# One layer-wide change in an encoder kernel: eight casts of w_out are issued behind the exponentials of the first head group

## The chip, the core and the metric

One core of a Trainium2 chip runs the whole program once. The metric is the device time of one execution in microseconds (us); the median of several runs counts. TensorE (PE) multiplies matrices, VectorE (DVE), ScalarE (ACT) and GpSimd (POOL) work element by element, and SyncE (SP) issues most of the loads and stores. Each engine takes its instructions strictly in the order in which they stand in its queue and waits for semaphores of the others.

## What is computed

The reference is a two-layer encoder over 1024 tokens of width 1024. Each layer mixes three groups of channels, and then applies a gated feed-forward network:

```python
y_f = _fourier_mix(zf, w_fourier[l])                       # 256 channels
y_a = _window_attn(q, k, v, sink[l])                       # 8 heads, 2 key heads, blocks of 128
y_m = _memory_attn(zm.reshape(b, s, N_MEM_HEADS, HEAD_DIM), km, vm)   # 4 heads, 256 memory rows
y = jnp.concatenate([_rmsnorm(y_f, gg[:256]), _rmsnorm(y_a, gg[256:768]), _rmsnorm(y_m, gg[768:])], -1) @ w_out[l]
x = x + _rmsnorm(y, g_post_mix[l])
gate, up = jnp.split(_rmsnorm(x, g_pre_ffn[l]) @ w_ffn_in[l], 2, axis=-1)
x = x + _rmsnorm((jax.nn.silu(gate) * up) @ w_ffn_out[l], g_post_ffn[l])
```

All inputs are 32-bit floats. Rows 256 to 767 of w_out (1024 x 1024) are those that the window attention's output is multiplied with.

## The kernel before

Every product is made from split operands: a matrix is cast to the shorter type that TensorE reads fast (`hi`) on ScalarE, and VectorE or GpSimd computes the remainder (`lo`); three matmuls then stand for one. The sequence is cut in 8 tiles of 128 tokens.

The code is written as lists of units that `weave` interleaves, and a scheduler then orders the instructions of each engine from a model of their durations; so the order on each engine is not that of the text. Large buffers are slices of two arenas (`arena_f` for 32-bit floats, `arena_r` for the short type) that the text places by hand, small ones and PSUM tiles come from pools.

The stages of a layer around the change, in order: the q projection woven with the memory attention (`mem_units`: score matmuls `ms`, VectorE row maxima L842, scaling of them L843, exponentials L846, reciprocals L850, GpSimd scaling of the probabilities L852, transposes `mpT`, casts L151 with remainders L152, products with the values `mav`, and their fold L876, L877); then the first head group of the window attention (`att_units(0)`: matmuls `sc`, masked maxima L729, four exponentials L741 and a small one for the sink L746, a GpSimd scaling L752, transposes `pT`, products `av`) woven with `fm_units`, which multiply the Fourier and memory parts with their rows of w_out (`mo`) and store the sums to `pmd`; then the second head group (`att_units(1)`) together with `out`, which multiplies the attention's output with rows 256 to 767 of w_out (also `mo`), adds `pmd` and goes on to the feed-forward network.

`load_wout` brings rows of w_out in: for each row block of 128 and each half of 512 columns one load (L909) into one of three buffers `raws`, one ScalarE cast with the gain (L910) and one VectorE pass for the remainder (L911). `fm_load` calls it for 4 row blocks that `fm_units` needs (tiles `big`), `out_load` for the row blocks 2 to 5, that is rows 256 to 767 (tiles in `arena_r`). Each call makes 8 loads, 8 casts and 8 passes. `values_32` (L791) rebuilds V for the second head group with two GpSimd additions; its output takes the place in `arena_f` of one of the buffers of `raws`.

Of the kernel before, what the change touches and what calls it, by code (L numbers as in the profile page):

```python
# [2 lines left out]

# [1 line left out]

# [10 lines left out]
AF = mybir.ActivationFunctionType  # L16
# [6 lines left out]
NT = S // P  # L23
# [35 lines left out]
def weave(*streams):  # L59

    order = []
    for si, units in enumerate(streams):
        order += [((i + 0.5) / len(units), si, i, u) for i, u in enumerate(units)]
    for *_, u in sorted(order, key=lambda o: o[:3]):
        u()
# [3 lines left out]
def tile_encoder(ctx: ExitStack, tc: tile.TileContext, T, C, out):  # L69
    nc = tc.nc  # L70
# [11 lines left out]
    def nm(s):  # L82
        uid[0] += 1
        return f"{s}_{uid[0]}"
# [15 lines left out]
    def at(k, *shape, dt=F32):  # L100

        o = int(k * 256)
        ap = arenas[F32R if dt is F32R else F32][:, o : o + math.prod(shape)]
        return shaped(ap.bitcast(dt) if dt is I32 else ap, shape)

    def big(*shape, dt=F32R):

        return bp.tile([P, *shape], dt, tag="big", name=nm("big"))
# [29 lines left out]
    def sm(n, name="v"):  # L138
        if name not in smp:
            smp[name] = ctx.enter_context(tc.tile_pool(name="sm_" + name, bufs=N_SM.get(name, 4)))  # L140
        return smp[name].tile([P, n], F32, tag=name, name=nm(name))

    def ps(shape, name="ps", tag="pd"):
        return psp[tag].tile([P] + list(shape), F32, tag=tag, name=nm(name))
# [323 lines left out]
    class Mix:  # L468
# [248 lines left out]
        def att_scores(self, g, n):  # L717
            k0, k1 = max(0, n - 1), min(NT, n + 2)
            W = (k1 - k0) * P
            m0 = (k0 - (n - 1)) * P  # L720
            half, c = divmod(n, 4)
            es_ = [es_ring(2, 3 * P) for _ in range(2)]
            rmax = sm(4, "rmax")
            for h in range(4):
                pt = ps([W], "sc", "sc")
                lhs = self.qst[half][h % 2][:, 2 * g + h // 2, c * P : c * P + P]
                for i in range(2):
                    mm(pt, lhs, self.kst[g][i][:, k0 * P : k1 * P], start=i == 0, stop=i == 1)  # L728
                nc.vector.tensor_tensor_reduce(  # L729
                    out=es_[h // 2][:, h % 2, :W], in0=pt, in1=mask[:, m0 : m0 + W], op0=ALU.add, op1=ALU.max,  # L730
                    scale=1.0, scalar=-3e38, accum_out=rmax[:, h : h + 1],
                )
            hs = slice(4 * g, 4 * g + 4)
            nmx = sm(4, "nmx")
            nc.vector.scalar_tensor_tensor(
                out=nmx, in0=rmax, scalar=-QK_SCALE, in1=nsink[:, self.l, hs], op0=ALU.mult, op1=ALU.min
            )
            den = sm(4, "den")
            for h in range(4):
                eh = es_[h // 2][:, h % 2, :W]  # L740
                nc.scalar.activation(  # L741
                    eh, eh, AF.Exp, bias=nmx[:, h : h + 1], scale=QK_SCALE, accum_out=den[:, h : h + 1]
                )
            es = sm(4, "es")
            nc.vector.tensor_tensor(out=es, in0=nmx, in1=psink[:, self.l, hs], op=ALU.add)
            nc.scalar.activation(es, es, AF.Exp)  # L746
            nc.vector.tensor_tensor(out=den, in0=den, in1=es, op=ALU.add)
            rden = sm(4, "rden")
            nc.vector.reciprocal(rden, den)
            for h in range(4):  # L750
                eh = es_[h // 2][:, h % 2, :W]
                nc.gpsimd.tensor_scalar(  # L752
                    out=eh, in0=eh, scalar1=rden[:, h : h + 1], scalar2=1.0, op0=ALU.mult, op1=ALU.mult
                )
            return es_
# [48 lines left out]
        def att_units(self, g):  # L804

            self.ya = getattr(self, "ya", {})
            st = {}

            def unit(i):
                if SKEW <= i < NT + SKEW:  # L810
                    n = i - SKEW
                    half, c = divmod(n, 4)
                    if g == 0 and n == 0:
                        ya = at(8, 2, 2, 512)
                        self.ya[0, 0], self.ya[0, 1] = ya[:, 0], ya[:, 1]
                    if g == 0:
                        dst = self.ya[g, half][:, :, c * P : c * P + P]
                    else:
                        dst = self.ya[g, n] = y1s(2, P)
                    self.att_values(g, n, st.pop(n), dst)  # L820
                    if g:
                        self.out_prep(n)
                if i < NT:
                    st[i] = self.att_scores(g, i)

            return [lambda i=i: unit(i) for i in range(NT + SKEW)]
# [69 lines left out]
            return [lambda i=i: unit(i) for i in range(n + 2)]  # L896


        def load_wout(self, ks, k0=None):

            res = {}
            for j, k in enumerate(ks):
                w = big(2, D) if k0 is None else at(k0 + 8 * j, 2, D, dt=F32R)
                hi, lo = w[:, 0], w[:, 1]
                g = ggT[:, self.l * NK + k : self.l * NK + k + 1]
                for n in range(2):
                    ns = slice(n * 512, n * 512 + 512)
                    raw = raws(512)
                    nc.sync.dma_start(raw, T["w_out"][self.l, k * P : (k + 1) * P, ns])  # L909
                    nc.scalar.activation(hi[:, ns], raw, AF.Copy, scale=g)  # L910
                    nc.vector.scalar_tensor_tensor(  # L911
                        out=lo[:, ns], in0=raw, scalar=g, in1=f32(hi[:, ns]), op0=ALU.mult, op1=ALU.subtract
                    )
                res[k] = (hi, lo)
            return res
# [59 lines left out]
            return [lambda t=t: unit(t) for t in range(NT)]  # L975

        def out_load(self):
            self.woa = self.load_wout((2, 3, 4, 5), 32)

        def out_gains(self):  # L980
            self.gpost = gain(T["g_post_mix"][self.l], at(48, D))
# [321 lines left out]
    mix = Mix(0, hT, mem)  # L1303
# [13 lines left out]
    for l in range(DEPTH):  # L1317
# [7 lines left out]
        mem.load()  # L1325
        weave(mix.mem_units(), q[4:8] + [mix.fm_load] + q[8:])
        fm = mix.fm_units(pmd)
        weave(mix.att_units(0), fm[:6] + [mix.out_load] + fm[6:])
        mix.out_gains()
        xs = x_in if l == 0 else x2d  # L1330
        hb = Blocks()
# [44 lines left out]
        if l + 1 < DEPTH:  # L1376
            mem = Memory(l + 1, 16, 0, 16, 28, "pT")
            mix = Mix(l + 1, nhT, mem)
# [76 lines left out]
```

## Time and profile before

| | us |
|---|---|
| median of 3 runs | 2131.66 |
| lowest and highest run | 2131.02, 2137.23 |
| profiled execution, its time | 2135.5 |
| its span in the trace | 2133.7 |
| TensorE busy | 2013.2 |
| VectorE, ScalarE, GpSimd busy | 1577.7, 1060.6, 863.4 |

The profiled execution is one run with the hardware profiler on; its span is what the trace covers. A busy share is an average over stages with different limits, so it is to be read by stage. The granted clock is a share of 2.4 GHz: 0.50 is the lower level of 1.2 GHz, and a mean between tells how much of a stretch ran at which.

### The profile page before, as it was taken

How to read it: one execution, taken by the hardware profiler on the slowest of the kernel's cores; microseconds unless marked ns; L12 is line 12 of the kernel's file. 1: busy time of each engine (PE TensorE's matmuls, PEld its weight loads, DVE VectorE, ACT ScalarE, POOL GpSimd, SP SyncE). 2: the span in 40 equal slices, each digit the busy share in tenths (PEclk: the TensorE clock that was granted, in tenths of full speed). 3: DMA queues.
4: the chain of work that ended last, by engine and by line, in shares of the span. 5: the costliest groups of instructions: out<-in, count | busy, mean ns of one | idle time of the engine just before them, and what ended most of it. 6: DMA issues, size and time to landing. Idle time of an engine off the chain costs nothing.

```text
span 2133.7 us, 28334 instructions
## 1 busy us (share of the span) xinstructions
PE 2013.2 (94%) x9490; PEld 1655.0 (78%) x9490; DVE 1577.7 (74%) x2441; ACT 1060.6 (50%) x2257; POOL 863.4 (40%) x858
## 2 busy tenths in 40 slices
PE   7998999699999999999989989996999999999997
PEld 6887887478888887878868768775888888878785
DVE  7568756898877877657875686578987787876774
ACT  6467776553333334444544677776433333345441
POOL 4244446653423434213453444475442333431322
PEclk9998999899999999999989989998999999999998
DMA  6112123422332326968731122243232232378874
GB/s 221 45 50 65 65 94 105 152 65 94 118 101 95 112 94 194 318 221 287 246 138 41 60 64 85 75 137 110 84 129 94 94 111 92 123 249 284 276 261 138
DMA packets 173602, 287.50 MB, mean 135 GB/s; under 512 B 15480, under 2 KB 73360, under 8 KB 173456
## 3 DMA queue, kind: packets, MB, share of 16 engines
q1 hardware_dynamic: 165392, 266.82, 38.1%
q10 hardware_dynamic: 8064, 18.88, 2.3%
q8 instruction: 74, 1.21, 0.2%
q14 instruction: 72, 0.59, 0.1%
HBM read 219.06 MB, written 66.58 MB: 134 GB/s over the span
## 4 chain that ended last, share of the span: by engine, by line
PE 74%; DMA 8%; DVE 7%; ACT 4%; POOL 4%; issue 2%; SPq 0%; POOLq 0%; DVEq 0%; ACTq 0%
PE fo L1232 12%; PE qz L1104 11%; PE qx L1104 11%; PE qy L1104 11%; PE mo L162 7%; PE qw L1104 5%; PE kvp L162 4%; PE qp L162 3%; DVE arena_r L152 3%; DMA arena_f<-actd 2%; PE sc L728 2%; PE pT L765 2%; DMA arena_f<-in_w_ffn_out 1%; ACT arena_r L151 1%; PE zT L162 1%
## 5 line engine op out<-in xcount | busy, mean ns | idle before, releaser
L151 ACT CAST arena_r<-arena_f 128x512 fp32r<-128x512 f32 (+1 forms) x780 | 443.1, 591 | 674.0 <-PE qz L1104 115.5
L152 DVE TENSOR_TENSOR arena_r<-arena_f,arena_r 128x512 fp32r<-128x512 f32 (+1 forms) x676 | 536.6, 816 | 182.9 <-ACT arena_r L151 179.6
L1232 PE MATMUL fo<-arena_r 128*128 128x512 f32 x1848 | 432.2, 395 | 17.5 <-ACT arena_r L151 15.1
L1232 PEld LDWEIGHTS fo<-arena_r 128*128 128x128 f32 x1848 | 351.7, 191 | 94.6 <-ACT arena_r L151 17.7
L1104 PE MATMUL qy<-arena_r 128*128 128x512 f32 x1056 | 261.5, 397 | 27.6 <-ACT arena_r L151 16.5
L1104 PEld LDWEIGHTS qy<-arena_r 128*128 128x128 f32 x1056 | 201.5, 192 | 72.0 <-ACT arena_r L151 17.0
L1094 DVE TENSOR_TENSOR arena_f<-arena_f 128x512 f32<-128x512 f32 x220 | 206.0, 939 | 5.1
L1104 PE MATMUL qz<-arena_r 128*128 128x512 f32 x704 | 196.3, 389 | 1.8 <-DVE arena_r L152 1.8
L1124 POOL TENSOR_TENSOR arena_f<-arena_f 128x512 f32<-128x512 f32 x44 | 73.0, 1658 | 292.8 <-ACT arena_f L1109 292.8
L1216 POOL TENSOR_TENSOR arena_f<-arena_f 128x512 f32<-128x512 f32 x50 | 73.6, 1475 | 269.5 <-DVE arena_r L152 136.2
L1104 PEld LDWEIGHTS qz<-arena_r 128*128 128x128 f32 x704 | 132.0, 188 | 29.8 <-DVE arena_r L152 2.4
L1156 POOL TENSOR_TENSOR arena_f<-arena_f 128x512 f32<-128x512 f32 x44 | 73.6, 1674 | 165.6 <-DVE arena_f L1136 119.1
L152 POOL TENSOR_TENSOR arena_r<-arena_f,arena_r 128x256 fp32r<-128x256 f32 (+2 forms) x104 | 88.8, 859 | 118.4 <-ACT arena_r L151 93.3
L1104 PE MATMUL qx<-arena_r 128*128 128x512 f32 x528 | 127.7, 389 | 1.4 <-ACT arena_r L151 1.4
L1104 PE MATMUL qw<-arena_r 128*128 128x512 f32 x528 | 127.6, 389 | 0.0
L1104 PE MATMUL qx<-big,arena_r 128*128 128x512 f32 x528 | 126.8, 389 | 0.0
L1104 PEld LDWEIGHTS qx<-arena_r 128*128 128x128 f32 x528 | 99.1, 188 | 22.5 <-ACT arena_r L151 2.0
L1104 PE MATMUL qz<-big,arena_r 128*128 128x512 f32 x352 | 115.5, 389 | 0.0
L1104 PEld LDWEIGHTS qw<-arena_r 128*128 128x128 f32 x528 | 99.1, 188 | 20.8
L1104 PEld LDWEIGHTS qx<-big,arena_r 128*128 128x128 f32 x528 | 99.1, 188 | 20.6
L162 PE MATMUL mo<-arena_r 128*128 128x512 f32 x384 | 102.6, 406 | 5.5 <-POOL arena_r L152 4.0
L162 PE MATMUL mo<-big,arena_r 128*128 128x512 f32 x384 | 102.3, 404 | 0.0
(223 smaller groups left out, 3558.1 us busy)
## 6 DMA issues: line engine op xcount, KB each, us to landing
arena_f<-in_w_ffn_out SPq DMA_DIRECT2D x264, 256.0 KB, 4.3
arena_f<-in_w_ffn_in SPq DMA_DIRECT2D x88, 512.0 KB, 3.6
actd<-arena_f SPq DMA_DIRECT2D x154, 256.0 KB, 3.7
arena_f<-actd SPq DMA_DIRECT2D x154, 256.0 KB, 4.2
arena_f<-in_w_in SPq DMA_DIRECT2D x40, 256.0 KB, 2.7
arena_f<-in_x SPq DMA_DIRECT2D x16, 512.0 KB, 4.1
arena_f<-in_w_out SPq DMA_DIRECT2D x32, 256.0 KB, 2.8
pmd<-arena_f ACTq DMA_DIRECT2D x32, 256.0 KB, 2.0
```

Source lines behind the costliest of these rows:

```text
L151: nc.scalar.copy(hi, src)
L152: return (lo_eng or nc.vector).tensor_tensor(out=lo, in0=src, in1=f32(hi), op=ALU.subtract)
L162: mm(self.dst, a, b, start=self.i == 0, stop=self.i == self.n - 1)
L728: mm(pt, lhs, self.kst[g][i][:, k0 * P : k1 * P], start=i == 0, stop=i == 1)
L765: nc.tensor.transpose(pT[:, h, :], es_[h // 2][:, h % 2, j * P : j * P + P], ident)
L1094: nc.vector.tensor_tensor(out=s, in0=a, in1=b, op=op)
L1104: mm(pt, a, b, start=start and n == 0, stop=n == 11, skip_group_check=not start)
L1124: nc.gpsimd.tensor_tensor(out=self.v, in0=self.v, in1=self.s2, op=ALU.add)
L1156: (G if i in (0, 3) else V).tensor_tensor(out=a[i], in0=c, in1=g[i], op=ALU.mult)
L1216: (nc.vector, nc.gpsimd)[k % 2].tensor_tensor(out=s, in0=x, in1=y, op=op)
L1232: mm(pt, ab[:, 0, x, sl], ab[:, 1, y], start=new and first and j == 0, stop=last and j == 2, skip_group_check=not new)
```

## The change

`att_scores` keeps the last of the four exponentials of each unit in `self.exps`; `load_wout` takes a list of such instructions and orders cast number 2j + n behind the one of unit 2j + n on ScalarE, without a semaphore (`issue_after` only fixes the order of two instructions of one engine). `out_load` passes the eight exponentials of head group 0; as these must exist by then, it is called behind the woven units and no longer between them, which also shifts the weave of the `fm` units by a little.

```diff
@@ -738,9 +738,10 @@
             den = sm(4, "den")
             for h in range(4):
                 eh = es_[h // 2][:, h % 2, :W]
-                nc.scalar.activation(
+                ex = nc.scalar.activation(
                     eh, eh, AF.Exp, bias=nmx[:, h : h + 1], scale=QK_SCALE, accum_out=den[:, h : h + 1]
                 )
+            self.exps[g, n] = ex
             es = sm(4, "es")
             nc.vector.tensor_tensor(out=es, in0=nmx, in1=psink[:, self.l, hs], op=ALU.add)
             nc.scalar.activation(es, es, AF.Exp)
@@ -804,6 +805,7 @@
         def att_units(self, g):
 
             self.ya = getattr(self, "ya", {})
+            self.exps = getattr(self, "exps", {})
             st = {}
 
             def unit(i):
@@ -896,7 +898,8 @@
             return [lambda i=i: unit(i) for i in range(n + 2)]
 
 
-        def load_wout(self, ks, k0=None):
+        def load_wout(self, ks, k0=None, behind=None):
+
 
             res = {}
             for j, k in enumerate(ks):
@@ -907,7 +910,8 @@
                     ns = slice(n * 512, n * 512 + 512)
                     raw = raws(512)
                     nc.sync.dma_start(raw, T["w_out"][self.l, k * P : (k + 1) * P, ns])
-                    nc.scalar.activation(hi[:, ns], raw, AF.Copy, scale=g)
+                    with tc.issue_after(behind[2 * j + n].ins) if behind else nullcontext():
+                        nc.scalar.activation(hi[:, ns], raw, AF.Copy, scale=g)
                     nc.vector.scalar_tensor_tensor(
                         out=lo[:, ns], in0=raw, scalar=g, in1=f32(hi[:, ns]), op0=ALU.mult, op1=ALU.subtract
                     )
@@ -975,7 +979,7 @@
             return [lambda t=t: unit(t) for t in range(NT)]
 
         def out_load(self):
-            self.woa = self.load_wout((2, 3, 4, 5), 32)
+            self.woa = self.load_wout((2, 3, 4, 5), 32, [self.exps[0, n] for n in range(NT)])
 
         def out_gains(self):
             self.gpost = gain(T["g_post_mix"][self.l], at(48, D))
@@ -1325,7 +1329,8 @@
         mem.load()
         weave(mix.mem_units(), q[4:8] + [mix.fm_load] + q[8:])
         fm = mix.fm_units(pmd)
-        weave(mix.att_units(0), fm[:6] + [mix.out_load] + fm[6:])
+        weave(mix.att_units(0), fm)
+        mix.out_load()
         mix.out_gains()
         xs = x_in if l == 0 else x2d
         hb = Blocks()
```

What this does to the queues is seen in the order of the built programs. First ScalarE in the memory attention of layer 0, near its end. `L846` of before and `L848` of the change are the memory exponentials, `L910` with `arena_r` the casts in question, `mpT` and `mav` as above. Before:

```order
L846 ACTIVATE arena_f,den_1902<-ms_1903,nmx_1901 128x256 x2
L910 ACTIVATE arena_r<-arena_f,const 128x512 x3
L876 COPY arena_f<-mav_1927 64x512
L910 ACTIVATE arena_r<-arena_f,const 128x512
L151 CAST arena_r<-mpT_1934 128x512
L846 ACTIVATE arena_f,den_1902<-ms_1912,nmx_1901 128x256 x2
L151 CAST arena_r<-mpT_1941 128x512
L910 ACTIVATE arena_r<-arena_f,const 128x512
L846 ACTIVATE arena_f,den_1950<-ms_1951,nmx_1949 128x256 x2
```

and with the change:

```order
L848 ACTIVATE arena_f,den_1902<-ms_1903,nmx_1901 128x256 x2
L151 CAST arena_r<-mpT_1849 128x512
L151 CAST arena_r<-mpT_1856 128x512
L151 CAST arena_r<-mpT_1934 128x512
L848 ACTIVATE arena_f,den_1902<-ms_1912,nmx_1901 128x256 x2
L151 CAST arena_r<-mpT_1941 128x512
L878 COPY arena_f<-mav_1927 64x512
L848 ACTIVATE arena_f,den_1950<-ms_1951,nmx_1949 128x256 x2
```

The five casts that stood here are gone from this place, as are three above it. VectorE at the same place (`L911` is the pass behind a cast, `L842` and `L844` are row maxima, `L843` and `L845` their scaling), before:

```order
L152 TENSOR_TENSOR arena_r<-mpT_1856,arena_r 128x512
L911 SCALAR_TENSOR_TENSOR arena_r<-arena_f,const,arena_r 128x512 x2
L842 TENSOR_REDUCE rmax_1900<-ms_1912 128x2
L911 SCALAR_TENSOR_TENSOR arena_r<-arena_f,const,arena_r 128x512
L843 TENSOR_SCALAR nmx_1901<-rmax_1900 128x2
L842 TENSOR_REDUCE rmax_1948<-ms_1951 128x2
L877 TENSOR_TENSOR arena_f<-mav_1927,arena_f 64x512
L843 TENSOR_SCALAR nmx_1949<-rmax_1948 128x2
L911 SCALAR_TENSOR_TENSOR arena_r<-arena_f,const,arena_r 128x512
L152 TENSOR_TENSOR arena_r<-mpT_1934,arena_r 128x512
L850 RECIPROCAL rden_1921<-den_1902 128x4
```

and with the change:

```order
L152 TENSOR_TENSOR arena_r<-mpT_1856,arena_r 128x512
L844 TENSOR_REDUCE rmax_1900<-ms_1912 128x2
L844 TENSOR_REDUCE rmax_1948<-ms_1951 128x2
L845 TENSOR_SCALAR nmx_1901<-rmax_1900 128x2
L152 TENSOR_TENSOR arena_r<-mpT_1934,arena_r 128x512
L845 TENSOR_SCALAR nmx_1949<-rmax_1948 128x2
L852 RECIPROCAL rden_1921<-den_1902 128x4
L152 TENSOR_TENSOR arena_r<-mpT_1941,arena_r 128x512
```

The passes are gone, and the two row maxima of `ms_1912` and `ms_1951` follow each other directly. GpSimd there, where `rden` marks the scaling of probabilities by the reciprocals, before:

```order
L852 TENSOR_SCALAR arena_f<-arena_f,rden_1836 128x256 x4
L791 TENSOR_TENSOR arena_f<-arena_r 128x256 x2
L852 TENSOR_SCALAR arena_f<-arena_f,rden_1921 128x256 x4
L852 TENSOR_SCALAR arena_f<-arena_f,rden_1969 128x256 x4
L929 TENSOR_TENSOR grs_2114<-ms_2109,const 128x1
```

and with the change:

```order
L854 TENSOR_SCALAR arena_f<-arena_f,rden_1836 128x256 x4
L854 TENSOR_SCALAR arena_f<-arena_f,rden_1921 128x256 x4
L854 TENSOR_SCALAR arena_f<-arena_f,rden_1969 128x256 x4
L477 MEMSET arena_r 128x1024
L753 TENSOR_SCALAR arena_f<-arena_f,rden_2092 128x256 x4
```

The two additions of `values_32` (L791) stood between two scalings and now stand later, behind the seventh unit of the first head group. Last, ScalarE at the first units of that head group (`den_2080` is unit 0, `den_2204` unit 1, `es` the sink's exponential), before:

```order
L741 ACTIVATE arena_f,den_2080<-arena_f,nmx_2078 128x256 x4
L746 ACTIVATE es_2088<-es_2088 128x4
L922 ACTIVATE arena_f<-arena_f 128x256
L741 ACTIVATE arena_f,den_2204<-arena_f,nmx_2202 128x384 x4
L746 ACTIVATE es_2209<-es_2209 128x4
L876 COPY arena_f<-mav_2054 64x512
```

and with the change:

```order
L741 ACTIVATE arena_f,den_2080<-arena_f,nmx_2078 128x256 x4
L914 ACTIVATE arena_r<-arena_f,const 128x512
L388 CAST arena_r<-qT_2045 64x4x128
L747 ACTIVATE es_2088<-es_2088 128x4
L878 COPY arena_f<-mav_2054 64x512
L741 ACTIVATE arena_f,den_2204<-arena_f,nmx_2202 128x384 x4
L914 ACTIVATE arena_r<-arena_f,const 128x512
L388 CAST arena_r<-qT_2045 64x4x128
L747 ACTIVATE es_2209<-es_2209 128x4
```

One cast (`L914`) now follows the four exponentials of each unit and stands ahead of the small one. In SyncE's queue of layer 0, fifteen w_out loads stand together as before, and the sixteenth now follows the first load of x and that of g_post_mix. Layer 1 is changed in the same way.

## Rows read from the trace of the kernel before

**Rows 1.** The page, part 1: busy time, share of the span, instructions of each engine.

```profile
PE 2013.2 (94%) x9490; PEld 1655.0 (78%) x9490; DVE 1577.7 (74%) x2441; ACT 1060.6 (50%) x2257; POOL 863.4 (40%) x858
```

**Rows 2.** Busy time by stretches; columns in the first row, PEclk is TensorE's granted clock.

```profile
core 0: us, PE busy (x) PEld busy (x) DVE busy (x) ACT busy (x) POOL busy (x), PEclk, DMA share, GB/s
...
198.00:214.00 16.00, 13.40 (x57) 10.92 (x57) 14.31 (x27) 13.47 (x36) 7.53 (x14) 0.71 0.31 98
...
209.00:217.00 8.00, 7.52 (x30) 6.25 (x31) 6.21 (x17) 6.69 (x21) 5.35 (x10) 0.57 0.01 2
...
222.00:230.00 8.00, 7.74 (x29) 6.97 (x30) 3.87 (x17) 5.27 (x19) 3.83 (x7) 0.57 0.00 1
...
230.00:300.00 70.00, 70.00 (x377) 59.74 (x376) 48.13 (x146) 50.08 (x133) 30.01 (x51) 1.00 0.30 106
...
1257.00:1272.00 15.00, 12.17 (x59) 9.12 (x58) 14.41 (x29) 13.81 (x37) 9.97 (x14) 0.88 0.35 106
...
1286.00:1350.00 64.00, 64.00 (x346) 54.73 (x344) 40.38 (x122) 45.26 (x123) 26.26 (x45) 1.00 0.29 100
```

**Rows 3.** Groups of instructions, 198 to 213 us: busy and mean ns, idle before.

```profile
L911 DVE SCALAR_TENSOR_TENSOR arena_r<-arena_f,const,arena_r 128x512 fp32r<-128x512 f32 x8 | 6.8, 849 | 0.5 <-ACT arena_r L910 0.5
...
L910 ACT ACTIVATE arena_r<-arena_f,const 128x512 fp32r<-128x512 f32 x8 | 5.7, 728 | 1.7 <-DMA arena_f<-in_w_out 1.7
```

**Rows 4.** TensorE in order of time, layers 0 and 1: start, duration, [idle before].

```profile
203.96 0.64 PE L840 MATMUL ms<-arena_r 128*128 128x256 f32 x4
...
209.35 0.80 PE L873 MATMUL mav<-arena_r 128*128 128x512 f32 x1 [2.47 <-ACT arena_r L151]
...
1262.91 0.64 PE L840 MATMUL ms<-arena_r 128*128 128x256 f32 x4
```

**Rows 5.** VectorE in order of time, layer 0.

```profile
200.51 1.26 DVE L911 SCALAR_TENSOR_TENSOR arena_r<-arena_f,const,arena_r 128x512 fp32r<-128x512 f32 x1
...
204.09 1.86 DVE L911 SCALAR_TENSOR_TENSOR arena_r<-arena_f,const,arena_r 128x512 fp32r<-128x512 f32 x2 [0.32 <-ACT arena_r L910]
...
205.86 0.68 DVE L842 TENSOR_REDUCE rmax<-ms 128x2 f32<-128x512 f32 x1
...
206.46 0.74 DVE L911 SCALAR_TENSOR_TENSOR arena_r<-arena_f,const,arena_r 128x512 fp32r<-128x512 f32 x1
...
207.12 0.16 DVE L843 TENSOR_SCALAR nmx<-rmax 128x2 f32<-128x2 f32 x1
```

**Rows 6.** ScalarE in order of time, layer 0.

```profile
207.97 0.72 ACT L910 ACTIVATE arena_r<-arena_f,const 128x512 fp32r<-128x512 f32 x1 [0.91 <-DMA arena_f<-in_w_out]
...
209.20 0.48 ACT L846 ACTIVATE arena_f<-ms,nmx 128x256 f32<-128x256 f32 x1
...
210.11 0.59 ACT L151 CAST arena_r<-mpT 128x512 fp32r<-128x512 f32 x1
```

**Rows 7.** GpSimd in order of time, layers 0 and 1.

```profile
209.56 1.42 POOL L791 TENSOR_TENSOR arena_f<-arena_r 128x256 f32<-128x256 f32 x2 [4.94 <-DVE arena_r L911]
...
210.96 2.28 POOL L852 TENSOR_SCALAR arena_f<-arena_f,rden 128x256 f32<-128x256 f32 x4
...
1268.72 3.43 POOL L852 TENSOR_SCALAR arena_f<-arena_f,rden 128x256 f32<-128x256 f32 x4
...
1274.82 1.85 POOL L852 TENSOR_SCALAR arena_f<-arena_f,rden 128x256 f32<-128x256 f32 x4 [2.67 <-DVE rden L850]
```

**Rows 8.** SyncE, ScalarE and TensorE in order of time, end of the first head group, layer 0.

```profile
247.28 0.33 SPq L214 DMA_DIRECT2D arena_f<-in_g_post_mix  x1
...
296.42 0.49 ACT L741 ACTIVATE arena_f<-arena_f,nmx 128x256 f32<-128x256 f32 x1
...
303.06 1.63 PE L162 MATMUL mo<-arena_r 128*128 128x512 f32 x6
```

**Rows 9.** The chain that ended last, in order of time.

```profile
346.77 2.55 DVE arena_r L152
...
353.27 1.55 POOL arena_f L752 x3
```

More of the change, by code (lines that the diff above doesn't have):

```diff
@@ L1 @@
 import math
-from contextlib import ExitStack
+from contextlib import ExitStack, nullcontext
 import numpy as np
```

## The prediction

> **What bounds the kernel now.** I read the page's engine table first: TensorE is busy for 94% of the span [rows 1], so what counts is where it stands still or runs at its lower clock. The table by stretches shows where the change can reach. In layer 0 the memory attention ends between 198 and 214 us: TensorE is busy for 13.4 of 16 us at a mean granted clock of 0.71, while VectorE has 14.3 and ScalarE 13.5 of 16 us. Here the vector-like engines set the pace. From 230 to 300 us, the first head group of the window attention woven with the products of the Fourier and memory parts, TensorE is busy for all 70 us at full clock, with VectorE at 48 and ScalarE at 50 us. Layer 1 has the same two stages (a clock of 0.88 from 1257 to 1272, then 64 of 64 us) [rows 2]. The list of one engine's instructions in time shows what the first stage waits for. The eight ScalarE casts of w_out's rows 256 to 767 (L910) take 5.7 us and wait 1.7 us for their loads; the eight VectorE passes behind them (L911) take 6.8 us [rows 3]. On TensorE, the product of probabilities and values stands 2.47 us behind ScalarE at 209.35 [rows 4].
>
> **The change, part by part.** The arithmetic is the same: 8 casts, 8 passes and 8 loads a layer leave the memory stage and return one by one behind the last exponential of each unit of the first head group.
>
> *Taken away, layer 0.* I follow one chain: the score product whose matmuls end at 203.96 + 0.64 = 204.60 [rows 4]. Before, VectorE then holds two w_out passes (204.09, 1.86 us), the row maximum (205.86), another pass (206.46, 0.74 us) and the scaling of the maximum (207.12) [rows 5]; ScalarE is still casting w_out at 207.97 and starts the exponentials only at 209.20; the next instruction is at 210.11 [rows 6]. GpSimd, moreover, has the two additions that rebuild V (L791) in front of the scaling of the probabilities. Their output lies where one of the three w_out load buffers does, so they wait 4.94 us for that pass and run from 209.56; the scaling starts at 210.96 and ends 2.28 us later, at 213.24 [rows 7]. In the new order (the VectorE rows shown with the change) two row maxima of 0.68 us and a 0.16 us step lie between 204.60 and the exponentials: 206.1. With 0.91 us for the exponentials and 0.2 for the reciprocal the scaling starts at 207.2; at its undisturbed 1.85 us [rows 7] it ends at 209.05. Gain 4.2 us.
>
> *Layer 1.* The same matmuls end at 1262.91 + 0.64 = 1263.55 [rows 4]; by the same steps the scaling starts at 1266.2 and ends at 1268.05. Before it started at 1268.72 and took 3.43 us [rows 7]: 1272.15. Gain 4.1 us. Sum 8.3 us. Its bounds: nothing, if this chain is not the one that ends last; at most what ScalarE gives to the casts with their waits, 7.4 us a layer [rows 3], or 14.8 us.
>
> *Added.* Each unit's cast (0.73 us, rows 3 give the mean) stands between the last exponential and the small exponential of the sink, which the sum of that unit waits for; behind it are queued the reciprocal, the four GpSimd scalings and the transposes. For units 1 to 7 I cost this at nothing, because TensorE is busy for 70 of 70 us in that stage [rows 2]: it has Fourier and memory products to do while a unit waits. For the first unit there is no cover yet, since TensorE idles and runs slowly before 230: 0.73 us a layer, 1.5 us in all. Without cover for the others too it would be 16 times 0.73 = 11.7 us. The eight passes (0.85 us mean) find 22 us of free VectorE time in the stage.
>
> *Loads.* The buffer ring of three lets the next load go only when a pass is done, so the loads now spread over the stage. In SyncE's queue the last one stands behind the loads of x and g_post_mix; in the old run g_post_mix was issued at 247.28, and the last cast's place is behind the exponential of 296.42. The first matmul with these weights starts at 303.06 [rows 8]. Some 6 us are left for cast and pass (1.5 us): cost 0. Were this cover gone, the price is what the pass is late, about 1 us a layer.
>
> *Clock.* TensorE has 0.57 mean clock in 209 to 217 and again in 222 to 230 [rows 2], right behind the waits that shrink. If the first of these stretches ran at 2.4 GHz instead, 8 us with a share of (1 - 0.57)/0.5 = 0.86 at half speed would give back 3.4 us; if nothing changes, 0. Which of the two cannot be read; layer 1 has less to win. I take 1.0 us, near the lower bound, since the casts of the other eight w_out tiles, ahead in the same stage, stay where they are and so do the waits that they make.
>
> **Weighing a rule against it.** The passes have two inputs in SBUF, and one that ran beside GpSimd work took 1.26 us (200.51) against 0.74 us [rows 5]; the GpSimd scaling that fell among them took 3.43 us against 1.85 [rows 7]. The Trainium skill, page "GPSIMD Engine Reference", section 1 (Specifications), says that GpSimd's SBUF interfaces are shared with VectorE and that vector instructions with two SBUF inputs contend for them; the trace agrees, with these numbers. The change carries that contention into a stage where GpSimd works 30 of 70 us [rows 2]: a rival below.
>
> **Sum.** 8.3 - 1.5 + 1.0 = 7.8 us off. The profiled execution took 2135.5 us, 1.8 us more than its span, and would come to 2127.7; the median of the three runs is 2131.66, 3.8 us lower, and I forecast that median: 2131.66 - 7.8 = **2123.9 us**. A measurement of this kernel can tell about 0.3%, 6.4 us, from no change.
>
> **Rivals.**
> - *The clock comes back as well.* Shorter waits keep TensorE at 2.4 GHz at both stretches of 0.57 in layer 0: 3.4 us each, less the 1.0 counted, so 5.8 us more: 2118.1 us. For it: the slow stretches follow waits. Against: layer 1 runs at 0.88 through the same waits, so it is not the waits alone. The Trainium skill, "TensorE: Matmul & The Clock Gate", section on HAM oscillation, states that idle gaps throttle the array and sustained work releases it; the trace agrees, and by that rule this rival is what one would expect, if the remaining gaps are short enough.
> - *The lead is lost later.* From 346 us the chain that ends last leaves TensorE for the softmax of the second head group, on VectorE, ScalarE and GpSimd (a GpSimd scaling of 1.55 us for three of four heads at 353.27) [rows 9]. The whole order behind the change is dealt anew; if one unit more stands in a row there, about 3 us a layer come back: 6 us, 2129.9 us.
> - *Contention* (the rule above). Each of the 16 passes 0.52 us longer and each of 16 scalings up to 1.58 us: 33.6 us of engine time. If a fifth of it reaches the path, 6.7 us: 2130.6 us.
> - *Slower: the cast in the unit's chain.* If TensorE's other work does not cover the units, each is later by the cast and, for the next unit's maximum, by the pass: 0.73 + 0.74 = 1.47 us, times 16 = 23.5, less 8.3: 2146.9 us. It turns slower by more than 0.3% when a unit costs TensorE over (7.8 + 6.4)/16 = 0.89 us. Against: not one of the 70 us was idle.
> That the casts stay where they were is excluded: the order shows them moved.
>
> **Chances.** Forecast 0.46 (0.06 of it under 6.4 us), clock 0.14, lost later 0.20, contention 0.09, slower 0.11. Faster: 0.40 + 0.14 = 0.54; same: 0.06 + 0.29 = 0.35; slower 0.11. For 8 in 10 the range reaches from the clock case with 1.6 us beyond it to just above the median of before: 2116.5 to 2132.5. The forecast's own range is 2120 to 2128.
>
> **What would show it.** Right: no L914 row between the memory exponentials; the V rebuild on GpSimd no longer waits for a pass in that stage; TensorE at full busy share from about 226 in layer 0 and 1281 in layer 1; 70 of 70 us still busy behind that; the first w_out product some 4 us earlier. Wrong: TensorE waits for transposes or probabilities of the first head group, or the stretch from 350 to 440 us grows by what was won.

## The result, and the profile after

| | before | changed |
|---|---|---|
| median, us | 2131.02 (13 runs) | 2138.3 (13 runs) |
| lowest and highest run | 2127.62, 2137.23 | 2135.16, 2140.04 |
| ratio, 95% interval | | 1.0028 (1.002 to 1.0037) |
| profiled execution, its span | 2135.5, 2133.7 | 2136.76, 2133.9 |

The change makes the kernel 0.28% slower, where 2123.9 us was forecast. The two profiled executions hide it: that of before lies 4.5 us above its median, that of the changed kernel 1.5 us below. So the two spans cannot be subtracted, and the traces must be read stage by stage. The engine table hardly moves (compare [rows 1]):

```profile
PE 2006.2 (94%) x9490; PEld 1648.7 (77%) x9490; DVE 1586.5 (74%) x2441; ACT 1060.8 (50%) x2257; POOL 855.9 (40%) x858
```

The table by stretches of the changed kernel, for the stretches of [rows 2] and one more, shows a stage that got better, one that got worse right behind it, and one far away:

```profile
core 0: us, PE busy (x) PEld busy (x) DVE busy (x) ACT busy (x) POOL busy (x), PEclk, DMA share, GB/s
198.00:214.00 16.00, 14.47 (x72) 10.98 (x73) 11.03 (x28) 11.38 (x36) 8.24 (x17) 0.89 0.07 21
209.00:217.00 8.00, 6.90 (x40) 5.14 (x40) 6.66 (x21) 6.06 (x19) 2.79 (x7) 1.00 0.00 1
222.00:230.00 8.00, 4.96 (x22) 4.34 (x21) 5.16 (x18) 4.47 (x12) 5.59 (x10) 0.55 0.19 68
230.00:300.00 70.00, 69.74 (x366) 58.92 (x365) 49.68 (x140) 52.01 (x136) 29.58 (x47) 0.98 0.34 113
1257.00:1272.00 15.00, 13.59 (x73) 10.04 (x73) 10.40 (x26) 11.26 (x33) 5.55 (x13) 1.00 0.00 0
1286.00:1350.00 64.00, 63.58 (x342) 54.09 (x341) 47.07 (x137) 47.44 (x123) 27.77 (x44) 1.00 0.33 110
1430.00:1490.00 60.00, 40.00 (x167) 30.54 (x166) 51.93 (x66) 33.98 (x69) 34.06 (x32) 0.80 0.37 123
```

and the last stretch before:

```profile
1430.00:1490.00 60.00, 42.87 (x191) 32.54 (x191) 52.54 (x65) 35.86 (x70) 37.82 (x36) 0.86 0.41 132
```

TensorE runs at full clock now at the memory attention's end (0.57 became 1.00 in 209 to 217, 0.88 became 1.00 in layer 1). The dense stretches stay dense. But TensorE has only 4.96 us of work in 222 to 230, where it had 7.74, still at 0.55; and in layer 1 it does 2.9 us less between 1430 and 1490.

To measure a layer free of what other layers did, I take the time from the first score product of its memory attention (`ms`) to the first product of the second feed-forward matrix (`fo`). TensorE's rows before:

```profile
141.17 0.40 PE L840 MATMUL ms<-arena_r 128*128 128x256 f32 x2
...
843.09 2.88 PE L1232 MATMUL fo<-arena_r 128*128 128x512 f32 x12
...
1196.34 0.36 PE L840 MATMUL ms<-arena_r 128*128 128x256 f32 x1
...
1893.05 5.60 PE L1232 MATMUL fo<-arena_r 128*128 128x512 f32 x24
```

and with the change:

```profile
141.83 0.40 PE L842 MATMUL ms<-arena_r 128*128 128x256 f32 x2
...
843.39 2.88 PE L1236 MATMUL fo<-arena_r 128*128 128x512 f32 x12
...
1192.89 0.36 PE L842 MATMUL ms<-arena_r 128*128 128x256 f32 x1
...
1894.77 5.60 PE L1236 MATMUL fo<-arena_r 128*128 128x512 f32 x24
```

Layer 0 took 843.09 - 141.17 = 701.92 us and takes 701.56; layer 1 took 696.71 and takes 701.88. So by these marks nothing is won in layer 0, and 5.2 us are lost in layer 1. The marks leave a stretch out: from layer 0's first `fo` to layer 1's first `ms` the change took 349.50 us and before 353.25. It took 353.25 to 354.57 us in the three kernels of this document whose layer 0 is that of before, and 347.48 to 352.06 us in the eleven others. One trace of each does not tell how much of that is the edit and how much the execution.

**Where layer 0's gain went.** GpSimd's scaling of memory probabilities, the end of the chain that I followed, in the changed kernel:

```profile
208.09 1.85 POOL L854 TENSOR_SCALAR arena_f<-arena_f,rden 128x256 f32<-128x256 f32 x4 [4.68 <-DVE rden L852]
...
223.08 2.28 POOL L753 TENSOR_SCALAR arena_f<-arena_f,rden 128x256 f32<-128x256 f32 x4 [2.47 <-ACT arena_f L741]
```

The first row ends at 209.94 instead of 213.24 [rows 7]. This execution had started the layer 0.66 us later, so 4.0 us are won. The second row is the scaling of the window attention's first unit. ScalarE and VectorE ahead of it:

```profile
217.97 0.50 ACT L741 ACTIVATE arena_f<-arena_f,nmx 128x256 f32<-128x256 f32 x1
...
218.47 0.71 ACT L914 ACTIVATE arena_r<-arena_f,const 128x512 fp32r<-128x512 f32 x1
219.20 0.58 ACT L388 CAST arena_r<-qT 64x512 fp32r<-64x512 f32 x1
219.69 0.20 ACT L747 ACTIVATE es<-es 128x4 f32<-128x4 f32 x1
```

```profile
219.24 0.74 DVE L915 SCALAR_TENSOR_TENSOR arena_r<-arena_f,const,arena_r 128x512 fp32r<-128x512 f32 x1
...
220.80 0.17 DVE L748 TENSOR_TENSOR den<-den,es 128x4 f32<-128x4 f32 x1
...
222.75 0.17 DVE L750 RECIPROCAL rden<-den 128x4 f32<-128x4 f32 x1
```

The last exponential ends at 218.47. The cast and another cast (L388, which the scheduler put beside it) hold the sink's exponential to 219.69; VectorE does the w_out pass and a queue of other work before the denominators (220.80) and the reciprocal (222.75). The scaling starts 4.6 us behind the last exponential. TensorE's queue adds to it: a small product (`ssp`) ahead of the transposition waits 1.53 us for VectorE's remainder of the next such cast (L389), and the transposition another 1.08 us for GpSimd:

```profile
225.42 0.98 PE L929 MATMUL ssp<-const,arena_f 128*128 128x2 f32 x4 [1.53 <-DVE arena_r L389]
227.49 1.94 PE L766 MATMUL pT<-const,arena_f 128*128 128x128 f32 x8 [1.08 <-POOL arena_f L753]
...
230.50 4.07 PE L162 MATMUL mo<-big,arena_r 128*128 128x512 f32 x12
```

The same unit before, on ScalarE, GpSimd and TensorE:

```profile
222.09 0.49 ACT L741 ACTIVATE arena_f<-arena_f,nmx 128x256 f32<-128x256 f32 x1
...
225.09 1.85 POOL L752 TENSOR_SCALAR arena_f<-arena_f,rden 128x256 f32<-128x256 f32 x4
...
228.34 1.71 PE L765 MATMUL pT<-const,arena_f 128*128 128x128 f32 x8
...
230.60 1.55 PE L162 MATMUL mo<-big,arena_r 128*128 128x512 f32 x6
```

There the scaling starts 2.5 us behind the exponentials and the transposition 5.8 us behind; with the change 4.6 and 9.0. The exponentials are 4.1 us earlier, the next large product (`mo`) 0.1 us: the first unit gave all of it back. The clock then makes it worse: that product begins at the low level, 12 matmuls in 4.07 us, where 6 took 1.55.

**Where layer 1 lost.** The memory attention won here as well; the scaling that I followed is now:

```profile
1262.42 1.85 POOL L854 TENSOR_SCALAR arena_f<-arena_f,rden 128x256 f32<-128x256 f32 x4 [2.71 <-DVE rden L852]
```

VectorE, GpSimd and TensorE at the last unit of the second head group, with the change:

```profile
1423.40 1.75 DVE L324 SCALAR_TENSOR_TENSOR arena_f<-arena_f,rrs 128x1024 f32<-128x1024 f32 x1 [1.40 <-POOL rrs L210]
1425.08 0.41 DVE L729 CUSTOM_DVE_ANT_0 arena_f<-sc,const 128x256 f32<-128x256 f32 x1
...
1425.49 0.41 DVE L729 CUSTOM_DVE_ANT_0 arena_f<-sc,const 128x256 f32<-128x256 f32 x1
...
1425.94 1.67 DVE L735 SCALAR_TENSOR_TENSOR nmx<-rmax,const 128x4 f32<-128x4 f32 x1
```

```profile
1425.24 2.35 POOL L325 TENSOR_TENSOR arena_f<-arena_f 128x1024 f32<-128x1024 f32 x1 [1.16 <-DVE arena_f L324]
...
1433.58 4.34 POOL L753 TENSOR_SCALAR arena_f<-arena_f,rden 128x256 f32<-128x256 f32 x4
```

```profile
1434.17 0.44 PE L766 MATMUL pT<-const,arena_f 128*128 128x128 f32 x2 [2.41 <-POOL arena_f L753]
```

and the answering rows before:

```profile
1422.97 0.16 DVE L735 SCALAR_TENSOR_TENSOR nmx<-rmax,const 128x4 f32<-128x4 f32 x1
...
1430.01 1.86 POOL L752 TENSOR_SCALAR arena_f<-arena_f,rden 128x256 f32<-128x256 f32 x4
```

No w_out cast is near this place. The edit is the same in both layers, but VectorE's order here is not that of before: the residual scaling of the fifth token tile (L324), itself waiting 1.40 us, now stands between the second and the third masked maximum (L729) of the last unit. Behind it GpSimd starts its addition for that tile (L325), and the tiny step `nmx`, 0.16 us before, takes 1.67. The scaling of the probabilities then starts at 1433.58 instead of 1430.01 and takes 4.34 us instead of 1.86, although this execution had entered the layer 3.45 us earlier.

Counting a layer's 384 `mo` products in the traces puts sizes on both places. Measured from the start of layer 1, the 24th product ends at 91.7 us before and at 91.8 with the change: the lead of the memory attention is gone in layer 1's first units as it was in layer 0. The 192nd, the last of the first head group, ends at 162.4 and 161.3, the last of the second head group at 253.3 and 258.8. So it is the second head group that became longer, 97.5 us instead of 90.9.

### The profile page after: what moved, and what is told of

It reads as the page before. It is cut to its first block, busy times and chain, and to the rows that moved or that the text cites. A ratio compares the mean times of both kernels' runs of the same rounds, so it can differ in the third digit from the quotient of the medians.

```text
span 2133.9 us, 28352 instructions
## 1 busy us (share of the span) xinstructions
PE 2006.2 (94%) x9490; PEld 1648.7 (77%) x9490; DVE 1586.5 (74%) x2441; ACT 1060.8 (50%) x2257; POOL 855.9 (40%) x858
## 4 chain that ended last, share of the span: by engine, by line
PE 73%; DVE 7%; DMA 7%; POOL 5%; ACT 4%; issue 3%; SPq 0%; POOLq 0%; DVEq 0%; ACTq 0%
PE fo L1236 12%; PE qx L1108 11%; PE qz L1108 11%; PE qy L1108 10%; PE mo L162 6%; PE qw L1108 5%; PE kvp L162 4%; PE qp L162 3%; DVE arena_r L152 3%; DMA arena_f<-actd 3%; PE sc L728 2%; PE pT L766 1%; PE zT L162 1%; ACT arena_r L151 1%; PE av L781 1%
## 5 line engine op out<-in xcount | busy, mean ns | idle before, releaser
L152 POOL TENSOR_TENSOR arena_r<-arena_f,arena_r 128x256 fp32r<-128x256 f32 (+2 forms) x104 | 83.7, 811 | 107.8 <-ACT arena_r L151 98.2
```

Source lines behind the costliest of these rows:

```text
L152: return (lo_eng or nc.vector).tensor_tensor(out=lo, in0=src, in1=f32(hi), op=ALU.subtract)
```

## The experiments

The theory: the change wins in the memory attention, gives it back in the first unit, and loses in layer 1 because the last unit is ordered otherwise. The rivals: each moved cast has a price; or the place of the casts costs as such. The code shown is cut to the lines that matter, and what stands behind # is added here. The kernels ran in several groups, each beside before, whose median lay between 2131.02 and 2132.59; the ratios are within a group. The two columns at the right are layer times as defined above, one trace each. Layers in which nothing was changed came to 701.92, 700.82 and 701.40 (layer 0) and to 696.71, 696.20 and 696.39 (layer 1), so about 1 us is noise; stages within an unchanged layer differ by up to 2 us. A layer time is not the total: the sum of the two and the timed ratio can differ by 5 us (layer1_only: 2.5 us more than before by the layers, 7.7 by the ratio).

| kernel | median, us | ratio to before, 95% interval | layer 0 | layer 1 |
|---|---|---|---|---|
| before | 2131.02 | 1 | 701.92 | 696.71 |
| the change | 2138.3 | 1.0028 (1.002 to 1.0037) | 701.56 | 701.88 |
| layer0_only | 2129.66 | 0.999 (0.9981 to 0.9999) | 701.33 | 696.20 |
| layer1_only | 2137.9 | 1.0036 (1.0021 to 1.0051) | 700.82 | 700.33 |
| no_pin | 2138.58 | 1.0026 (1.0014 to 1.0037) | 701.43 | 702.74 |
| from_unit1 | 2127.84 | 0.9984 (0.9976 to 0.9993) | 698.20 | 695.48 |
| before_late_maxima | 2135.32 | 1.0014 (1.0002 to 1.0026) | 701.40 | 698.50 |
| change_early_maxima | 2145.39 | 1.0066 (1.0052 to 1.008) | 703.06 | 710.16 |
| behind_sink | 2132.27 | 1.0003 (0.9994 to 1.0013) | 696.13 | 703.08 |
| from_unit1_twice | 2135.96 | 1.0021 (1.0009 to 1.0032) | 701.58 | 703.30 |
| change_late_residual | 2132.28 | 1.0002 (0.9993 to 1.001) | 701.60 | 699.02 |
| mixed_places | 2134.19 | 1.0006 (0.9995 to 1.0017) | 697.70 | 701.94 |
| old_weave | 2131.57 | 1.0006 (0.9996 to 1.0017) | 700.40 | 701.16 |
| layer0_behind_sink | 2124.84 | 0.9968 (0.9957 to 0.9979) | 697.68 | 696.39 |

**One layer at a time.**

```diff
+        if l == 0:                       # layer1_only: l == 1
             weave(mix.att_units(0), fm)
             mix.out_load()
+        else:
+            weave(mix.att_units(0), fm[:6] + [mix.out_load] + fm[6:])
```

> The change is made in layer 0 alone; layer 1 keeps the old place of the casts. Stage theory (each layer's loss is where its own trace shows it): in the trace of the changed kernel layer 0 wins about 4 us in the memory attention, gives them back between 216 and 230 us and ends level, so this kernel is within 2 us of the one before, and layer 1 runs as before. Rival, a price per cast: half of the 7.3 us that the whole change lost, so about +3.6 us.

> The change is made in layer 1 alone. Stage theory: layer 1 lost 5.2 us between 1255 and 1530 us in the changed kernel's trace, nearly all in the last units of the second head group, so this kernel is 4 to 7 us slower than before. Rival, a price per cast: about +3.6 us, as much as layer 0 alone.

Layer 0 alone is not slower (0.999); layer 1 alone has the whole loss (1.0036). A price per cast falls: the same eight casts cost nothing in one layer and 6 to 8 us in the other.

**The casts back in the old place.**

```diff
-            self.woa = self.load_wout((2, 3, 4, 5), 32, [self.exps[0, n] for n in range(NT)])
+            self.woa = self.load_wout((2, 3, 4, 5), 32)
```

> The loads, casts and passes are called behind the woven units as in the change, but not ordered behind the exponentials; the built order has the eight casts back among the memory exponentials. If the place of the casts is what costs, this is the time of before, within 2 us. If the shift of the woven units and the order that the scheduler then makes of the second head group costs, it is 4 us or more slower than before, with the loss behind 1420 us.

The casts are where they were before, and the kernel is as slow as the change: 1.0026, with layer 1 at 702.74. VectorE and GpSimd at the last unit:

```profile
1424.90 1.75 DVE L324 SCALAR_TENSOR_TENSOR arena_f<-arena_f,rrs 128x1024 f32<-128x1024 f32 x1 [1.40 <-POOL rrs L210]
...
1427.43 1.67 DVE L735 SCALAR_TENSOR_TENSOR nmx<-rmax,const 128x4 f32<-128x4 f32 x1
```

```profile
1426.73 2.36 POOL L325 TENSOR_TENSOR arena_f<-arena_f 128x1024 f32<-128x1024 f32 x1 [1.16 <-DVE arena_f L324]
```

Those are the rows of the change. So the place of the casts is not needed for layer 1's loss; calling them behind the woven units, which also shifts the weave, is enough to make the scheduler choose that order.

**No cast in the first unit.**

```diff
-[self.exps[0, n] for n in range(NT)]
+[self.exps[0, min(n + 1, NT - 1)] for n in range(NT)]
```

> As the change, but cast n is ordered behind the exponentials of unit n+1 (the last two behind unit 7), so the first unit has no cast and no pass in its way. Theory of the first unit: TensorE had nothing else to do there, and cast and pass made its probabilities some 3 us later in each layer; then this kernel keeps about 3 us a layer more than the change: 6 us faster than it, level with before. Rival (the loss comes from the second head group alone): the first unit's gain shows at 230 us but the total stays 4 to 8 us above before.

3.8 us under the before of its group by the medians, 3.4 by the ratio (0.9984), and so more than expected. In layer 0, ScalarE, GpSimd and TensorE at the first unit:

```profile
218.67 0.50 ACT L741 ACTIVATE arena_f<-arena_f,nmx 128x256 f32<-128x256 f32 x1
...
221.28 1.85 POOL L753 TENSOR_SCALAR arena_f<-arena_f,rden 128x256 f32<-128x256 f32 x4
...
222.04 0.38 PE L766 MATMUL pT<-const,arena_f 128*128 128x128 f32 x2
...
227.59 1.55 PE L162 MATMUL mo<-big,arena_r 128*128 128x512 f32 x6
```

The scaling starts 2.1 us behind the last exponential (the change: 4.6), the transposition 2.9 (9.0), and `mo` runs at full clock. Layer 0 keeps 3.7 us to its end. In layer 1 the 24th `mo` product ends at 87.5 us, 4.3 us ahead of the change, so its first units keep the lead too. The end of layer 1 is not a clean reading of the first unit, because its last unit is here again in the order of before.

**The order of the last unit, put into the kernel before.**

```diff
+late = (self.l, g, n, h // 2) == (1, 1, NT - 1, 1)
+with tc.issue_after(scaled[0].ins) if late else nullcontext():   # the fifth tile's L324
     nc.vector.tensor_tensor_reduce(...)
```

> The kernel before, casts where they were, with one order taken from the changed kernel: in layer 1 the last two masked maxima of the last unit of the second head group stand behind VectorE's scaling of the fifth token tile's residual. If this order is what the change lost in layer 1 (its trace lost 5 to 7 us between 1430 and 1480 us), this kernel is 4 to 7 us slower than before. If the loss came from the casts or from their place, it is within 2 us of before.

Slower by 0.14% (3.0 us by the ratio; the interval reaches from 0.4 to 5.5). Its layer 1 grows by 1.8 us in the trace, less than expected; its second head group, from the 192nd `mo` product to the last, by 4.0 us (94.9). The tiny step behind the residual scaling is late again:

```profile
1428.21 2.24 DVE L739 SCALAR_TENSOR_TENSOR nmx<-rmax,const 128x4 f32<-128x4 f32 x1
```

```profile
1428.05 2.38 POOL L327 TENSOR_TENSOR arena_f<-arena_f 128x1024 f32<-128x1024 f32 x1
```

**That order taken out of the change.** Two attempts. The first delayed the whole step of the fifth tile:

```diff
+if l == 1 and i == 7:
+    with tc.issue_after(mix.nmx.ins):
+        hs[4] = mix.out(4, x1d[4])
```

> The changed kernel with that order undone: in layer 1 the residual scaling of the fifth token tile is ordered behind the last unit's maxima. If the order is the cause, 4 to 7 us faster than the change: 2131 to 2134 us, level with before. If the casts are the cause, it stays at 2137 to 2139 us.

It is 14 us slower than before and tells nothing of the order: the step now also stood behind the preparation of the seventh tile, which takes the fifth tile's place in a ring of two buffers. So in layer 1 the fifth tile is multiplied from the seventh tile's operands, which is another computation, and its products need that tile's softmax first. The second attempt delayed only the residual scaling and what follows it:

```diff
+if (l, i) == (1, 7):
+    with tc.issue_after(mix.nmx.ins):
+        hs[4][0]()          # L324 and the addition
+    hs[4] = hs[4][1]()      # the normalization
```

> The changed kernel with one order undone: in layer 1 the scaling of the fifth token tile's residual, its addition and its normalization are issued behind the last unit's maxima of the second head group instead of between them; all else of the tile stays in place. If that order is what cost the change its layer 1, the 4 to 7 us between 1430 and 1480 us mostly come back: 2131 to 2135 us. If another part of the tail's order does it, or the casts, the time stays at 2137 to 2139 us.

2132.28 us: level with before (1.0002), 5.5 us under the change by the two ratios, as expected. VectorE now:

```profile
1424.95 0.16 DVE L741 SCALAR_TENSOR_TENSOR nmx<-rmax,const 128x4 f32<-128x4 f32 x1
1425.03 1.28 DVE L326 SCALAR_TENSOR_TENSOR arena_f<-arena_f,rrs 128x1024 f32<-128x1024 f32 x1
```

Layer 0 is untouched (701.60). This one order is thus worth 3 us (put in) to 5.5 us (taken out) by the timed runs, and 1.8 to 2.9 us by the layer times of single traces; the second head group, 97.5 us with the change, takes 93.6 here, so 3.9 us of its 6.6 us are back.

**The cast behind the sink's exponential.**

```diff
-nc.scalar.activation(es, es, AF.Exp)
+self.exps[g, n] = nc.scalar.activation(es, es, AF.Exp)
```

> As the change, but each cast stands behind the sink's small exponential. The layer 1 order of the last unit is that of the change, so about 5 us are lost there. If the cast in front of the sink's exponential is what makes the first unit's probabilities late, most of the 5 us that the first unit gave back come back in each layer, and the kernel is near 2130 us; if it is the VectorE pass and the queue there, little comes back and the kernel stays at 2136 us or above.

In layer 0 this is as good as leaving the first unit free: 5.8 us shorter than before. With the cast later, its VectorE pass falls behind the unit's reciprocal as well (220.51 and 220.42). Layer 1 lost 6.4 us, in the last unit as foreseen and also in the first: TensorE waits for GpSimd and then runs a stretch at 1.2 GHz, as the rows of TensorE and of that stretch show:

```profile
1272.78 0.69 PE L765 MATMUL pT<-const,arena_f 128*128 128x128 f32 x2 [1.41 <-POOL arena_f L752]
1273.12 2.91 PE L162 MATMUL mo<-big,arena_r 128*128 128x512 f32 x6
```

```profile
1272.00:1276.00 4.00, 3.22 (x9) 2.54 (x10) 1.60 (x4) 3.76 (x12) 2.09 (x4) 0.50 0.38 132
```

The median, 2132.27, lies between the two cases of the expectation: the first unit's gain of one layer against the last unit's loss of the other.

**Twice the casts.** In from_unit1, each moved cast and pass is done twice:

```diff
+if behind:
+    with tc.issue_after(behind[2 * j + n].ins):
+        nc.scalar.activation(hi[:, ns], raw, AF.Copy, scale=g)
+    nc.vector.scalar_tensor_tensor(out=lo[:, ns], in0=raw, scalar=g, in1=f32(hi[:, ns]), op0=ALU.mult, op1=ALU.subtract)
```

> As the run without a cast in the first unit, with every moved cast and its VectorE pass done twice (the second writes the same values): 16 more casts (11.6 us of ScalarE) and 16 more passes (12 us of VectorE). If TensorE's own work covers the units, the stretches from 235 to 300 and 1300 to 1350 us grow by less than 1 us each; if a cast costs the path, by 0.7 us a unit, 5 us a layer.

In layer 1 TensorE is busy for all 64 of 64 us from 1286 to 1350 in both kernels. In layer 0, from 230 to 300 us, it is busy for 9.28 + 20.00 + 19.73 + 18.14 = 67.15 us instead of 10.00 + 20.00 + 20.00 + 19.58 = 69.58: 2.4 us for eight more casts and passes, more than the one and less than the other expectation. A window does not follow the work; the count of `mo` products does. From the 24th to the 192nd, the units with the doubled casts, layer 0 takes 72.5 us instead of 67.6, so 4.9 us more and near the price of a cast on the path, and layer 1 takes 69.0 instead of 68.8: covered. Layer 1 as a whole is 7.8 us longer all the same. 4.8 us of it are there by the 24th product (92.3 instead of 87.5), although no cast stands in the first unit, and the rest comes behind the 192nd, where the built order of the last units is a third one.

**Three mixtures.**

```diff
 # mixed_places
+[(self.exps[0, min(n + 1, NT - 1)] if self.l else self.sinks[0, n]) for n in range(NT)]
 # old_weave
+weave(mix.att_units(0), fm[:6] + [lambda: None] + fm[6:])
 # layer0_behind_sink: behind the sink in layer 0; layer 1 as before
+[self.exps[0, n] for n in range(NT)] if self.l == 0 else None
```

> Casts behind the sink's exponential of unit n in layer 0 and behind the exponentials of unit n+1 in layer 1; the built order of layer 1 has the last unit's maxima ahead of the residual scaling of the fifth tile. By the two theories together (first unit free, tail order as before) layer 0 wins 5 to 6 us and layer 1 1 to 3 us: 2122 to 2126 us, faster than both kernels. If the tail order is not what decides, layer 1 loses about 5 us as in the change: 2130 us.

> The change with an empty unit in the place where the casts' unit stood in the weave, so that the units keep their old places in the text. If the shift of the weave made the bad order in layer 1, this is 4 to 7 us faster than the change. But the built order has both residual scalings ahead of the last unit's scaled maximum here too; by the theory of the order it is then no faster than the change: 2136 us or more, the first unit of both layers as in the change.

> Casts behind the sink's exponential in layer 0 alone; layer 1 keeps the old place and, in the built order, the old order of its last unit. By the stage theory layer 0 is 5 to 6 us shorter than before (as in the run with casts behind the sink in both layers) and layer 1 as before: 2125 to 2127 us, faster than both kernels. If the shorter layer 0 was an accident of that run, or if it is lost behind the layer, the time is that of before.

mixed_places missed: layer 0 kept its gain (697.70), but layer 1 lost 5.2 us although the residual scaling stood behind the last unit's maxima. TensorE there:

```profile
1439.15 5.75 PE L162 MATMUL mo<-arena_r 128*128 128x512 f32 x24
1451.04 1.94 PE L1038 MATMUL hTp<-const,arena_f 128*128 128x128 f32 x8 [6.15 <-DVE arena_f L289]
```

The products are done at 1444.90, where those of before were done at 1449.66; but this execution had entered the layer 7.4 us earlier, and the transpositions behind them (`hTp`) wait 6.15 us for VectorE's normalization (L289). So the place of that one residual scaling is not a rule for the whole tail.

old_weave missed too. Its median is level with before (1.0006) and about 5 us under the change (1.0028), where the theory of the order wanted the time of the change. Yet its order is not that of before: in the trace L324 stands between the last unit's third and fourth maximum, `nmx` starts at 1427.71, and layer 1 takes 701.16. That trace is of its slowest execution (2138.42, the median 2131.57), so what layer 1 costs in a usual one is not shown. Of the change's loss, then, the shift of the weave may be a part, and a late `nmx` alone does not foretell the time.

layer0_behind_sink came nearly as expected: 2124.84 us, ratio 0.9968, faster than both kernels; its layer 0 is 4.2 us shorter than before, where 5 to 6 were expected, and its layer 1 is that of before to 0.3 us.

## Why the prediction was wrong

- *Taken away.* Right. Forecast 4.2 and 4.1 us; the scaling that I followed ends 4.0 us earlier in layer 0. In layer 1 it ends at 1264.27 instead of 1272.15; less the 3.45 us by which this execution started the layer earlier, 4.4 us.
- *Added, units 1 to 7 at nothing.* Right for the change: TensorE stays at 69.74 of 70 and 63.58 of 64 us, and from the 24th to the 192nd `mo` product layer 0 takes 1.2 us more than before and layer 1 1.2 us less. The cover is not large: twice the work costs 4.9 us in layer 0.
- *Added, the first unit at 0.73 us a layer.* This step failed first. From the last exponential to the transposition the chain grew from 5.8 to 9.0 us in layer 0, and all 4 us were gone at the first large product behind it. I had priced the cast alone. The order printed with the change already showed a second cast (L388) between it and the sink's exponential; and I did not follow VectorE, where the pass and a queue stood ahead of the denominators. Freeing the first unit (from_unit1) or putting the cast behind the sink's exponential (behind_sink, layer0_behind_sink) gives layer 0 back 3.4 us, and 3.9 to 5.4 us. In layer 1 the lead is gone by the 24th product as well; from_unit1 keeps it there, from_unit1_twice with the same places does not, so its cause there is open.
- *Loads, at nothing.* Right: in layer 0 the last pass is done at 291.03, and the first product with these weights starts at 305.42. That product was to come 4 us earlier; by the layer's start it comes 1.7 us later.
- *Clock, 1.0 us.* The first slow stretch went to 2.4 GHz, as the rival hoped, but TensorE was waiting in it (6.90 of 8 us busy, 7.52 before), so there was little to speed up. The second stayed at 0.55, and layer 1 has a slow stretch of its own now, 0.50 from 1280 to 1284.
- *Rival "the lead is lost later".* The right place with the wrong size and sign of the total: I gave it 3 us a layer and let it at most eat the gain. Layer 0 ends level, and its lead went in the first unit. Layer 1 ends 5.2 us behind: its second head group takes 6.6 us more, when the lead is already gone. That an order dealt anew can be worse than no lead I left out, and that closed the range at 2132.5. This is the second step that failed.
- *Contention.* It was there, but not where I put it: not at the w_out passes (0.77 and 0.81 us each in the two layers, 0.85 and 0.80 before), but at the last unit, where one small step waited for a GpSimd addition. That unit's scaling on GpSimd (4.34 us instead of 1.86) ran beside four VectorE instructions with two inputs in SBUF; that these held it is likely and not shown.
- *Slower, the cast in the unit's chain.* True for the first unit alone. Its 23.5 us for sixteen units did not happen.

The largest term of the sum came true, 8.4 us measured for 8.3, and did not help the total: it was given back in the first units, and a later stage lost more. What stays open: why the scheduler prefers the worse order once the call moves, and how layer 1's loss divides. 3 to 5.5 us hang on the residual scaling by the timed runs; mixed_places and from_unit1_twice show that other orders of the tail cost as much, and old_weave that a late last unit need not.

## What to carry to other kernels

Where a scheduler orders the queues, an edit has two effects, its own and the new order far behind it; here the second was the larger, and a control that makes only the second (no_pin: the call moved, the work left in place) showed it at once. Work that is covered by TensorE in a dense stage is not covered in the first unit of that stage: price the whole chain of the first unit, on each engine, to the first large product behind it. And the better place was behind the sink's exponential, in one layer only.

## What the hardware showed

A small VectorE instruction can take as long as the GpSimd instruction beside it has left. `nmx` (128x4, two inputs in SBUF) takes 0.16 us alone. Beside GpSimd's addition over 128x1024 it ended at 1425.94 + 1.67 = 1427.61 where that ended at 1425.24 + 2.35 = 1427.59; in no_pin at 1429.10 and 1429.09; in before_late_maxima at 1430.45 and 1430.43. The Trainium skill, "Trainium Architecture — The Big Picture", section "What this means for kernel authors", calls the port pair of VectorE and GpSimd an exclusive lock and not a split of bandwidth; the trace agrees, with these three pairs. A masked maximum (L729, one input in PSUM) at 1425.49, inside the first of these additions, took its usual 0.41 us. The hold is not peculiar to the change: in the two traces of before and of the change eleven `nmx` steps beside a GpSimd instruction take 0.26 to 2.36 us, and each ends within 0.03 us of that instruction's end.
